# Feed-forward of an encoder on Trainium2: tokens on partitions, 256x1024 weight tiles, and Strassen's seven products in tiles 4 and 6 of each eight

## The chip, the cores and the metric

The kernel runs on one core of one Trainium2 chip. The metric is the device time of one execution in microseconds. An execution of the kernel before takes 2321.56 us (median of 3 runs, 2321.46 to 2324.35).

## What is computed

An encoder of two layers over x of 256 tokens x 2048, all in float32. Each layer is a norm, an attention (layer 0: neighbourhood attention with 16 heads; layer 1: dilated attention with 3 groups of 8 heads), a norm, and a feed-forward with squared ReLU; a last norm follows. The change is in the feed-forward, which is there twice:

```python
def rms_norm(x, g):
    y = xf * lax.rsqrt(jnp.mean(xf * xf, axis=-1, keepdims=True) + EPS)
    return (y * g.astype(jnp.float32)).astype(x.dtype)

def sq_relu_mlp(h, w1, w2):
    return jnp.square(jax.nn.relu(h @ w1)) @ w2        # w1: 2048 x 8192, w2: 8192 x 2048
...
        g, w1, w2 = ffns[i]
        x = x + sq_relu_mlp(rms_norm(x, g), w1, w2)
```

## The kernel before

All weights stream through the core once, in 400 blocks of 512 x 512 (1 MB each); 256 of them are the feed-forwards'. A block is one Step of a list, which is the program: `quarters` issues its matmuls in four parts, `tasks` are other matmuls put after a quarter (scores, transposes), `evac` reads finished sums, `post` follows. SyncE's queue loads a block into one of three buffers `w` (`load(i + 5)` after step i). `prep` cuts it in two halves of 128 x 1024: ScalarE rounds w into `wh` (line 104), VectorE subtracts to get the rest `wl` (line 105); there are four buffers of each, two steps' worth, and step i issues the cutting for step i + 2. Each engine takes its instructions in the order written here. Activations are cut into two parts in the same way, and a product is wh with both parts of the activation and wl with the first.

There are two forms of product. `gemm_cols` (lines 134 and 136) holds the weights still and gives out[columns, tokens]: 16 pairs of one matmul with 512 columns (both parts of the tokens) and one with 256. `gemm_rows` with `products` (lines 155 to 157) holds the activations still and gives out[tokens, columns]: 24 matmuls of 512 columns. The feed-forward (`ffn`) goes through the 8192 hidden columns in four groups of 2048: 16 blocks of the first product by `gemm_cols`, whose result, after ReLU and square, is at once hT, the left side of the second product; then 16 blocks of the second by `gemm_rows`. Sums lie in three pairs of PSUM banks, and two single banks serve transposes and scores. A norm's transposes (line 194) turn x, four of 128 x 128 at a time. `rows_apart` and `finish` end the kernel: the first half of the tokens is finished while the second half is multiplied.

## Time and profile before

| | |
|---|---|
| median of the runs | 2321.56 us |
| profiled execution, first to last instruction (no other time of it is listed) | 2320.3 us |
| TensorE busy (matmul) | 2300.7 us, 99% |
| VectorE busy | 1406.0 us, 61% |
| ScalarE busy | 1092.6 us, 47% |
| GpSimd busy | 0.7 us |
| bytes moved by DMA | 430.36 MB, 185 GB/s |
| granted TensorE clock, mean | 0.999 |

The span is cut in stages: up to 407 us layer 0's attention, to 1120 us its feed-forward, to 1601 us layer 1's attention, then its feed-forward and the last norm. Matmuls are pipelined, so the time from the start of one to the start of the next tells what it costs in a stream, and its own duration tells how long its result takes.

### The profile page before, as it was taken

Reading aid. Unit: us, or ns where it says so; the run is one execution under the profiler, and the core shown is the slowest. Engines: PE = TensorE matmul, PEld = TensorE weight load, DVE = VectorE, ACT = ScalarE, POOL = GpSimd, SP = SyncE. Lnnn points to the kernel's source line nnn. Section 1 sums busy time; section 2 is a strip of 40 time slices with the busy share of each in tenths; the row PEclk is TensorE's granted clock in tenths of the full one; section 3 lists DMA queues with packets and bytes.
Section 4 is the critical chain, followed back from the end, with each engine's and each line's share of the span. In section 5 each row is a group of like instructions: output and inputs, shape, how many; then the busy total and the mean of one; then the engine's idle time right before and its main releaser. Section 6 shows DMA issues by size and latency. Waiting matters only on the chain.

```text
span 2320.3 us, 29178 instructions
## 1 busy us (share of the span) xinstructions
PE 2300.7 (99%) x11956; PEld 1963.1 (85%) x11956; DVE 1406.0 (61%) x1635; ACT 1092.6 (47%) x1390; POOL 0.7 (0%) x6
## 2 busy tenths in 40 slices
PE   8999999999999999999999999999999999999998
PEld 7888888888888888888888888888888888888886
DVE  6666765654555555566777667756654654555654
ACT  6444545543443453455444544445543543543443
POOL 0000000000000000000000000000000000000000
PEclk9999999999999999999999999999999999999999
DMA  7555655555555555555555545454555555555553
GB/s 248 169 175 176 191 182 170 182 197 200 182 187 194 185 196 189 193 181 188 189 179 184 177 164 181 164 181 169 191 192 193 182 200 187 189 187 200 200 192 135
DMA packets 73862, 430.36 MB, mean 185 GB/s; under 512 B 19776, under 2 KB 20352, under 8 KB 22528
## 3 DMA queue, kind: packets, MB, share of 16 engines
q1 hardware_dynamic: 73056, 426.80, 54.3%
q8 instruction: 93, 1.52, 0.3%
q10 hardware_dynamic: 672, 1.70, 0.2%
q14 instruction: 41, 0.34, 0.0%
HBM read 426.38 MB, written 2.10 MB: 185 GB/s over the span
## 4 chain that ended last, share of the span: by engine, by line
PE 98%; DMA 1%; DVE 1%; ACT 0%; issue 0%; SPq 0%; ACTq 0%; DVEq 0%
PE acc L134 33%; PE acc L136 17%; PE acc L156 15%; PE acc L155 15%; PE acc L157 15%; PE misc L194 1%; DMA bias<-in_rpb_dram 0%; PE misc L111 0%; PE misc L110 0%; PE misc L109 0%; DVE wl L105 0%; PE misc L593 0%; PE misc L553 0%; PE misc L380 0%; ACT wh L104 0%
## 5 line engine op out<-in xcount | busy, mean ns | idle before, releaser
L105 DVE TENSOR_TENSOR wl<-w,wh 128x1024 fp32r<-128x1024 f32 (+1 forms) x802 | 972.8, 1221 | 735.8 <-ACT wh L104 733.6
L104 ACT CAST wh<-w 128x1024 fp32r<-128x1024 f32 (+1 forms) x802 | 834.9, 1049 | 936.9 <-PE acc L157 460.2
L134 PE MATMUL acc<-xT,wh 128*128 128x512 f32 x3328 | 1178.5, 399 | 0.9 <-ACT wh L104 0.9
L136 PE MATMUL acc<-xT,wl 128*128 128x256 f32 x3328 | 935.0, 281 | 2.3 <-DVE wl L105 2.3
L134 PEld LDWEIGHTS acc<-xT,wh 128*128 128x128 f32 x3328 | 626.4, 188 | 150.4 <-ACT wh L104 1.9
L136 PEld LDWEIGHTS acc<-xT,wl 128*128 128x128 f32 x3328 | 629.8, 189 | 3.7 <-DVE wl L105 3.2
L155 PE MATMUL acc<-wh,hT 128*128 128x512 f32 x1024 | 399.5, 390 | 0.0
L156 PE MATMUL acc<-wl,hT 128*128 128x512 f32 x1024 | 399.0, 390 | 0.0
L157 PE MATMUL acc<-wh,hT 128*128 128x512 f32 x1024 | 398.9, 390 | 0.0
L157 PEld LDWEIGHTS acc<-wh,hT 128*128 128x128 f32 x1024 | 192.3, 188 | 39.9
L155 PEld LDWEIGHTS acc<-wh,hT 128*128 128x128 f32 x1024 | 192.3, 188 | 39.7
L156 PEld LDWEIGHTS acc<-wl,hT 128*128 128x128 f32 x1024 | 192.3, 188 | 39.4
L155 PE MATMUL acc<-wh,xT 128*128 128x512 f32 x320 | 126.7, 396 | 0.0
L156 PE MATMUL acc<-wl,xT 128*128 128x512 f32 x320 | 125.2, 391 | 1.1 <-DVE wl L105 1.1
L157 PE MATMUL acc<-wh,xT 128*128 128x512 f32 x320 | 124.9, 390 | 0.0
L144 ACT COPY b<-acc 128x512 f32<-128x512 f32 x104 | 60.7, 586 | 64.8 <-PE acc L136 59.1
L146 DVE TENSOR_TENSOR z<-acc,b 128x512 f32<-128x512 f32 x104 | 71.5, 691 | 25.8 <-ACT b L144 25.2
L155 PE MATMUL acc<-wh,oT 128*128 128x512 f32 x192 | 76.6, 399 | 0.0
L157 PE MATMUL acc<-wh,oT 128*128 128x512 f32 x192 | 75.0, 391 | 0.0
L156 PE MATMUL acc<-wl,oT 128*128 128x512 f32 x192 | 74.9, 390 | 0.0
L156 PEld LDWEIGHTS acc<-wl,xT 128*128 128x128 f32 x320 | 60.2, 188 | 13.1 <-DVE wl L105 1.8
L157 PEld LDWEIGHTS acc<-wh,xT 128*128 128x128 f32 x320 | 60.1, 188 | 12.5
(123 smaller groups left out, 1044.9 us busy)
## 6 DMA issues: line engine op xcount, KB each, us to landing
w<-in_ffn_w_dram SPq DMA_DIRECT2D x256, 1024.0 KB, 4.8
w<-in_dil_wqkv_dram SPq DMA_DIRECT2D x72, 1024.0 KB, 4.8
w<-in_na_wqkv_dram SPq DMA_DIRECT2D x47, 1024.0 KB, 4.9
w<-in_na_wo_dram SPq DMA_DIRECT2D x16, 1024.0 KB, 4.9
w<-in_dil_wo_dram SPq DMA_DIRECT2D x8, 1024.0 KB, 4.8
bias<-in_rpb_dram SPq DMA_DIRECT2D x32, 96.0 KB, 8.7
out_dram<-x SPq DMA_DIRECT2D x8, 256.0 KB, 2.5
x<-in_x_dram SPq DMA_DIRECT2D x3, 512.0 KB, 7.8
```

Of the source, the lines that this page charges most:

```text
L104: nc.scalar.copy(dst_hi, src)
L105: nc.vector.tensor_tensor(out=dst_lo, in0=src, in1=dst_hi.bitcast(F32), op=ALU.subtract)
L134: nc.tensor.matmul(o, s.hi[a // 2][:, a % 2, cs], xt.rearrange("p h t -> p (h t)"), start=first, stop=False)
L136: nc.tensor.matmul(o[:, :T], s.lo[a // 2][:, a % 2, cs], xt[:, 0, :], start=False, stop=last)
L144: nc.scalar.copy(b, acc[j][:, :, T:])
L146: nc.vector.tensor_tensor(out=z, in0=acc[j][:, :, :T], in1=b, op=ALU.add)
L155: nc.tensor.matmul(o, xh, wh, start=start, stop=False)
L156: nc.tensor.matmul(o, xh, wl, start=False, stop=False)
L157: nc.tensor.matmul(o, xl, wh, start=False, stop=stop)
L194: nc.tensor.transpose(self.tp[:, a, tb * P:(tb + 1) * P], x[:, tb, kt * P:(kt + 1) * P], ident)
```

## The change

Both products of the feed-forward now hold the activations still (tokens on partitions). A Step is a tile of 256 x 1024 weights, four blocks of 128 x 512 in `w`, loaded by two DMAs of 512 KB. Each group of 2048 hidden columns is four runs of eight such tiles: two runs for the first product, two for the second; a run (`gemm_pair`) sums 2048 x 1024 weights into up to eight PSUM banks. Its tiles are of kind "s" (24 matmuls, as `gemm_rows`) or, for tiles 4 and 6 of the eight (`FF_PAIRS`, counted from 0: 3 and 5), "x": Strassen's seven products (Winograd's form), 21 matmuls. For an x tile the activations have three sums more (`sums_and_parts`), the weights four: VectorE adds `sums`, ScalarE rounds them into `hs`, VectorE subtracts to get `ls` (`prep_x`). The products with sums go to four banks "1", "6", "7", "5", which `begin` puts together in C after the last x tile; `end` adds the four banks of the plain sums ("2", "4", "S", "3") in the last tile. After a run of the first product C holds the hidden values with tokens on partitions: ScalarE applies 1/rms with ReLU and the square during tile 0 of the next run (`squared_relu`), four groups of four transposes follow in its tiles 1 and 2 (into the spare banks), and hT is cut from them (`post`). In the first norm of a feed-forward 1/rms is no longer spread over columns. Sums, subtractions and C are VectorE's alone.

The rest of the diff gives the buffers other pools: eight banks as one PSUM tile, of which the attention uses six in pairs and two singly as before, and SBUF pools that are begun for the attention or the feed-forward. The core of it:

```diff
+    def prep(i, n):
         if i >= len(steps):
             return
         s = steps[i]
-        hi = hlpool.tile([P, 2, 512], F32R, name="wh", tag="wh")
-        lo = hlpool.tile([P, 2, 512], F32R, name="wl", tag="wl")
-        part = s.w[:, 2 * u:2 * u + 2, :]
-        if i:
-            split(hi, lo, part)
+        if s.kind == "x":
+            prep_x(s, n)
...
+    def prep_x(s, n):
+        w = s.w
+        if n == 0:
+            t = s.sums = part.pool.tile([P, 4, 512], F32, name="sums", tag="sums", bufs=1)
+            add(nc.vector, t[:, 0:2, :], w[:, 1:3, :], w[:, 0, :].unsqueeze(1).to_broadcast([P, 2, 512]))
+            add(nc.vector, t[:, 2, :], t[:, 1, :], w[:, 1, :])
+            add(nc.vector, t[:, 3, :], t[:, 2, :], w[:, 3, :])
+        elif n == 1:
+            hi, lo = two_parts(s, 1)
+            split(hi, lo, w[:, 2:4, :])
+            s.hs = part.pool.tile([P, 4, 512], F32R, name="hs", tag="hs", bufs=2)
+            nc.scalar.copy(s.hs, s.sums)
+        elif n == 2:
+            ls = part.pool.tile([P, 4, 512], F32R, name="ls", tag="ls", bufs=2)
+            subtract(nc.vector, ls, s.sums, s.hs.bitcast(F32))
+            for a in range(4):
+                s.hi[4 + a], s.lo[4 + a] = s.hs[:, a, :], ls[:, a, :]
         else:
-            for a in range(2):
-                split(hi[:, a], lo[:, a], part[:, a])
-        s.hi[u], s.lo[u] = hi, lo
+            hi, lo = two_parts(s, 0)
+            split(hi[:, 1, :], lo[:, 1, :], w[:, 1, :])
     def block(w, k, c):
...
+        order, ps.order = ps.order, ps.order[4:] + ps.order[:4]
+        ps.spare = order[4:]
+        return {q: order[n] for n, q in enumerate(("2", "4", "S", "3", "1", "6", "7", "5"))}
...
+    STD = {(0, 0): "2", (0, 1): "3", (1, 0): "4", (1, 1): "S"}
...
+        def product(bank, a, b, last):
+            if not q:
+                q.update({k: banks[:, n, :] for k, n in sum_banks().items()})
+            three(q[bank], a, b, bank not in touched, last)
+            touched.add(bank)
+        X = (("1", "A11", 2), ("2", "A12", 3), ("6", "S2", 6), ("7", "S3", 4), ("5", "S1", 5), ("4", "A22", 7),
+             ("3", "S4", 1))
...
+            loads = [(w[k, 2 * cp + c].rearrange("p (a n) -> p a n", n=512)[:, 2 * u:2 * u + 2, :],
+                      2 - 2 * c, 4 - 2 * c) for c in (1, 0)]
+            if kind == "x":
+                def quarter(s, m, pair=pair, n=n):
+                    for bank, a, b in X[2 * m:2 * m + 2]:
+                        product(bank, left(pair, a), (s.hi[b], s.lo[b]), n == first_x[-1] and bank in "1567")
+            else:
+                def quarter(s, m, pair=pair, n=n):
+                    tb, c = ((0, 0), (1, 0), (1, 1), (0, 1))[m]
+                    for kk in range(2):
+                        b = 2 * (1 - c) + kk
+                        a = (("A11", "A12"), ("A21", "A22"))[tb][kk]
+                        product(STD[tb, c], left(pair, a), (s.hi[b], s.lo[b]), n == len(order) - 1 and kk == 1)
+            s = Step(kind, loads, quarter)
...
+        def begin(m):
+            if m == 0:
+                C = q["C"] = part.pool.tile([P, 4, 512], F32, name="C", tag="C")
+                nc.scalar.copy(C[:, 0, :], q["1"])
+                q["U"] = scratch([P, 512], "U")
+                subtract(nc.vector, q["U"], q["6"], C[:, 0, :])
+            elif m == 1:
+                subtract(nc.vector, q["C"][:, 2, :], q["U"], q["7"])
+            elif m == 2:
+                add(nc.vector, q["C"][:, 1, :], q["U"], q["5"])
+            else:
+                add(nc.vector, q["C"][:, 3, :], q["C"][:, 2, :], q["5"])
+        def end(m):
+            C = q["C"]
+            if m == 0:
+                add(nc.vector, C[:, 0, :], C[:, 0, :], q["2"])
+            elif m == 1:
+                subtract(nc.vector, C[:, 2, :], q["4"], C[:, 2, :])
+            elif m == 2:
+                add(nc.vector, C[:, 3, :], C[:, 3, :], q["S"])
+            else:
+                add(nc.vector, C[:, 1, :], C[:, 1, :], q["3"])
+        s = made[first_x[-1] + 1]
+        for m in range(4):
+            s.after[m].append(lambda m=m: begin(m))
+            if not split_end:
+                made[-1].after[m].append(lambda m=m: end(m))
+        finish(made, q)
...
+    def sums_and_parts(raw, t, half, sums):
+        c = scratch([P, 3, P], "c")
+        a11, a21, a12, a22 = raw[:, 0, :P], raw[:, 0, P:], raw[:, 1, :P], raw[:, 1, P:]
+        subtract(nc.vector, c[:, 0, :], a11, a21)
+        subtract(nc.vector, a21, a21, a22)
+        subtract(nc.vector, c[:, 1, :], a11, a21)
+        subtract(nc.vector, c[:, 2, :], a12, c[:, 1, :])
+        hi, lo = (t[:, 2 * half:2 * half + 2, h, :] for h in range(2))
+        nc.scalar.copy(hi, raw)
+        nc.scalar.copy(sums[:, 0], c)
+        subtract(nc.vector, lo, raw, hi.bitcast(F32))
+        subtract(nc.vector, sums[:, 1], c, sums[:, 0].bitcast(F32))
...
+    FF_PAIRS = (3, 5)
+    FF_ORDER = [("x" if k in FF_PAIRS else "s", k) for k in range(8)]
+    FF_LAST = [FF_ORDER[k] for k in (0, 1, 3, 2, 5, 4, 6, 7)]
...
-                def done(zs, c=c, hT=hT):
-                    t = hT[c] = big.tile([P, 4, 2, T], F32R, name="hT", tag="big")
-                    for z in zs:
-                        nc.vector.scalar_tensor_tensor(
-                            out=z, in0=z, scalar=0.0, in1=norm.bc.unsqueeze(1).to_broadcast([P, 2, T]),
-                            op0=ALU.max, op1=ALU.mult)
-                        nc.scalar.activation(z, z, AF.Square)
-                    for j, z in enumerate(zs):
-                        split(t[:, 2 * j:2 * j + 2, 0, :], t[:, 2 * j:2 * j + 2, 1, :], z)
-                gemm_cols(w1, (4 * g + c) * 512, norm.xT, 4, done)
+            hT, sums = [None] * 4, {}
+            def hidden(made, q, cp, hT=hT, sums=sums):
...
+                def squared_relu(tb, n):
+                    c = q["C"][:, 2 * tb + n, :]
+                    nc.scalar.activation(c, c, AF.Relu, scale=norm.r[:, tb:tb + 1])
+                    nc.scalar.activation(c, c, AF.Square)
+                for m, (tb, n) in enumerate(((0, 0), (1, 0), (1, 1), (0, 1))):
+                    at_after(i, m, lambda tb=tb, n=n: squared_relu(tb, n))
+                for r in range(4):
+                    held = {}
+                    def pe(r=r, held=held):
+                        held["t"] = t = ps.misc()
+                        for a in range(2):
+                            f = 2 * r + a
+                            for tb in range(2):
+                                nc.tensor.transpose(t[:, a, tb * P:(tb + 1) * P],
+                                                    q["C"][:, 2 * tb + f // 4, f % 4 * P:(f % 4 + 1) * P], ident)
+                    def post(r=r, held=held):
+                        c, half, pair = 2 * cp + r // 2, r % 2, 4 * cp + r
+                        if half == 0:
+                            hT[c] = opool.tile([P, 4, 2, T], F32R, name="hT", tag="o")
+                        if pair in FF_PAIRS:
+                            raw = scratch([P, 2, T], "h")
+                            nc.scalar.copy(raw, held["t"])
+                            sums[pair] = part.pool.tile([P, 2, 3, P], F32R, name="hs", tag="hsum", bufs=len(FF_PAIRS))
+                            sums_and_parts(raw, hT[c], half, sums[pair])
+                        else:
+                            to = hT[c][:, 2 * half:2 * half + 2]
+                            split(to[:, :, 0, :], to[:, :, 1, :], held["t"])
+                    at(i + 1 + r // 2, pe, post, quarter=r % 2 * 2)
...
+                gemm_pair(w1, 2 * g + cp, norm.xT, norm.sums, FF_ORDER, lambda made, q, cp=cp: hidden(made, q, cp))
...
-            out_rows(w2g, hT, 4, next_norm if last else None, next_done if last else None)
...
+                def rows(tb):
+                    to = x[:, tb, cp * 1024:(cp + 1) * 1024]
+                    add(nc.vector, to, to, both(q, tb))
+                made[-1].evac.append(lambda: rows(1))
+                made[-1].evac.append(lambda: rows(0))
...
+            if i == 0 and n in (1, 2):
+                prep(1, 2 * n - 1)
+            elif i in (1, 2):
+                if n == 2:
+                    prep(i + 2, 1)
+            elif i and n < 3:
+                prep(i + 2, n)
...
-        prep(i + 2, 1)
+            prep(2, 1)
+        prep(i + 2, 3)
```

How this moves instructions, at three places. **VectorE, at the start of the second product of a group.** Before (hT is the last cut of the hidden values, line 105 `split`, line 271 the addition to x):

```order
L471 SCALAR_TENSOR_TENSOR z<-z,rbc 128x512 x2
L105 TENSOR_TENSOR hT<-z,hT 128x2x256 x2
L105 TENSOR_TENSOR wl<-w,wh 128x1024 x7
L271 TENSOR_TENSOR x<-x,acc 128x512 x2
L105 TENSOR_TENSOR wl<-w,wh 128x1024 x8
```

Now, in tiles 1 and 2 of the second product's first run, from `ls` of tile 3 on (line 133 subtracts, line 191 is `split`; c and h are the sums of the activations and their raw values, hs and hT here their two parts):

```order
L133 TENSOR_TENSOR ls<-sums,hs 128x2048
L133 TENSOR_TENSOR c<-h 128x128
L133 TENSOR_TENSOR h<-h 128x128
L133 TENSOR_TENSOR c<-h 128x128
L133 TENSOR_TENSOR c<-h,c 128x128
L133 TENSOR_TENSOR hT<-h,hT 128x2x256
L133 TENSOR_TENSOR hs<-c,hs 128x384
L191 TENSOR_TENSOR wl<-w,wh 128x512
L191 TENSOR_TENSOR hT<-banks,hT 128x2x256
L191 TENSOR_TENSOR wl<-w,wh 128x1024
L191 TENSOR_TENSOR hT<-banks,hT 128x2x256
L191 TENSOR_TENSOR wl<-w,wh 128x1024
```

Where VectorE had a cut of weights alone there now stands a 2048-column subtraction and six instructions on the activations, and the cut of the last transposes (the second hT out of banks) is behind all of them.

**ScalarE, at the same change from the first product to the second.** Before (line 474 is the square, 104 the casts):

```order
L474 ACTIVATE z<-z 128x512 x2
L104 CAST hT<-z 128x2x256 x2
L104 CAST wh<-w 128x1024 x39
```

Now, in tile 0 of the next run and the start of tile 1 (lines 681 and 682 are ReLU and square, 190 the casts, 176 the cast of the weight sums):

```order
L681 ACTIVATE C<-C,rstd 128x512
L682 ACTIVATE C<-C 128x512
L681 ACTIVATE C<-C,rstd 128x512
L682 ACTIVATE C<-C 128x512
L190 CAST wh<-w 128x1024
L681 ACTIVATE C<-C,rstd 128x512
L682 ACTIVATE C<-C 128x512
L681 ACTIVATE C<-C,rstd 128x512
L682 ACTIVATE C<-C 128x512
L190 CAST wh<-w 128x1024
L190 CAST hT<-banks 128x2x256
L190 CAST wh<-w 128x1024
```

The two casts of tile 2 stand behind four and behind eight passes over C.

**TensorE, in tile 3 of the second product's first run**, the first x tile, with the engines that each matmul waits for (lines 195 to 197 are `three`). Before, a block of the second product waits only for its weights:

```order
L155 MATMUL acc<-wh,hT 128x512 [waits Activation_49]
L156 MATMUL acc<-wl,hT 128x512 [waits DVE_49]
L157 MATMUL acc<-wh,hT 128x512
L155 MATMUL acc<-wh,hT 128x512
L156 MATMUL acc<-wl,hT 128x512
```

Now, from the third of the seven products on (banks "6", "7", "5", and the first of "4"):

```order
L195 MATMUL banks<-hs 128x512 [waits Activation_49]
L196 MATMUL banks<-ls,hs 128x512 [waits DVE_49]
L197 MATMUL banks<-hs 128x512
L195 MATMUL banks<-hs 128x512 [waits DVE_49]
L196 MATMUL banks<-ls,hs 128x512
L197 MATMUL banks<-hs 128x512
L195 MATMUL banks<-hs,hT 128x512 [waits DVE_49]
L196 MATMUL banks<-ls,hT 128x512
L197 MATMUL banks<-hs,hT 128x512
L195 MATMUL banks<-hs,hT 128x512
```

Product "6" waits for `hs` and `ls`; "7" and "5" each wait once more for VectorE, which frees their banks when it has cut the third and the fourth group of transposes.

## Rows read from the trace of the kernel before

**Rows 1.** The page's head: busy time by engine, granted clock by slice

```profile
span 2320.3 us, 29178 instructions
PE 2300.7 (99%) x11956; PEld 1963.1 (85%) x11956; DVE 1406.0 (61%) x1635; ACT 1092.6 (47%) x1390; POOL 0.7 (0%) x6
...
PEclk9999999999999999999999999999999999999999
```

**Rows 2.** Waits, whole span: who waited for whom, us in total, times, longest

```profile
ACT wh L104 <- PE acc L157: 460.2, 292, 2.2
ACT wh L104 <- PE acc L134: 452.4, 269, 3.5
...
PE acc L136 <- DVE wl L105: 2.3, 3, 0.8
PE acc L156 <- DVE wl L105: 1.1, 2, 0.6
```

**Rows 3.** Windows of the two feed-forward stages: busy time by engine, clock, DMA

```profile
407.00:1119.57 712.57, 712.57 (x3622) 605.45 (x3620) 406.27 (x421) 332.03 (x386) 0.00 (x0) 1.00 0.56 189
...
1601.35:2320.00 718.65, 709.96 (x3597) 602.94 (x3595) 403.05 (x417) 328.68 (x381) 0.00 (x0) 1.00 0.54 187
```

**Rows 4.** Timeline of TensorE at the edges of products: start us, us, what

```profile
584.27 0.39 PE L134 MATMUL acc<-xT,wh 128*128 128x512 f32 x1
...
674.71 0.40 PE L155 MATMUL acc<-wh,hT 128*128 128x512 f32 x1
...
761.78 0.39 PE L134 MATMUL acc<-xT,wh 128*128 128x512 f32 x1
...
1601.35 0.39 PE L134 MATMUL acc<-xT,wh 128*128 128x512 f32 x1
...
1691.56 0.39 PE L155 MATMUL acc<-wh,hT 128*128 128x512 f32 x1
```

**Rows 5.** Timeline of TensorE around four transposes (line 194)

```profile
376.12 0.60 PE L194 MATMUL misc<-ident,x 128*128 128x128 f32 x4
376.47 0.48 PE L155 MATMUL acc<-wh,oT 128*128 128x512 f32 x1
376.79 0.39 PE L156 MATMUL acc<-wl,oT 128*128 128x512 f32 x1
```

**Rows 6.** Groups by line and shape: count, busy us, mean ns, idle before

```profile
L105 DVE TENSOR_TENSOR wl<-w,wh 128x1024 fp32r<-128x1024 f32 x798 | 970.2, 1223 | 735.8 <-ACT wh L104 733.6
L104 ACT CAST wh<-w 128x1024 fp32r<-128x1024 f32 x798 | 832.6, 1051 | 936.9 <-PE acc L157 460.2 <-PE acc L134 452.4 <-issue 9.2
...
L105 DVE TENSOR_TENSOR hT<-z,hT 128x512 fp32r<-128x512 f32 x64 | 41.4, 689 | 38.7 <-ACT hT L104 38.7
...
L474 ACT ACTIVATE z<-z 128x512 f32<-128x512 f32 x64 | 39.5, 633 | 60.6 <-DVE z L471 60.6
...
L104 ACT CAST hT<-z 128x512 fp32r<-128x512 f32 x64 | 36.0, 610 | 0.0
...
L194 PE MATMUL misc<-ident,x 128*128 128x128 f32 x128 | 20.3, 283 | 5.9 <-DMA x<-in_x_dram 5.9
...
L105 DVE TENSOR_TENSOR oT<-misc,oT 128x256 fp32r<-128x256 f32 x16 | 6.7, 418 | 0.0
...
L690 ACT ACTIVATE x<-x,fr 128x512 f32<-128x512 f32 x4 | 2.7, 716 | 1.4 <-DVE fr L680 1.4
...
L260 DVE TENSOR_TENSOR ru<-ru,ms 128x2 f32<-128x2 f32 x4 | 0.7, 162 | 0.1
```

**Rows 7.** Timelines of VectorE and ScalarE: instructions that follow one another

```profile
436.04 1.29 DVE L105 TENSOR_TENSOR hT<-z,hT 128x512 fp32r<-128x512 f32 x2 [1.21 <-ACT hT L104]
437.52 2.36 DVE L105 TENSOR_TENSOR wl<-w,wh 128x1024 fp32r<-128x1024 f32 x2 [0.18 <-ACT wh L104]
...
436.44 2.00 ACT L104 CAST wh<-w 128x1024 fp32r<-128x1024 f32 x2
```

**Rows 8.** Timeline of the end: VectorE in `finish`

```profile
2305.91 0.69 DVE L669 TENSOR_TENSOR x<-x,acc 128x512 f32<-128x512 f32 x1 [3.13 <-PE acc L157]
...
2308.92 0.74 DVE L687 SCALAR_TENSOR_TENSOR x<-x,fr,gf 128x512 f32<-128x512 f32 x1
```

**Rows 9.** DMA issues: size, median us to landing

```profile
w<-in_ffn_w_dram SPq DMA_DIRECT2D x256, 1024.0 KB, 4.8
```

More of the change, by code (lines that the diff above doesn't have):

```diff
@@ L341, in qk @@
         def qk(self, which):
-            t = [mid.tile([P, 4, T], F32R, name="qk", tag="mid") for _ in range(2)]
+            t = [part.pool.tile([P, 4, T], F32R, name="qk", tag="mid", bufs=9) for _ in range(2)]
             setattr(self, which, t)
@@ L382, in s2_post @@
         def s2_post(self, h):
-            t = [tmp.tile([P, 2, T], F32R, name="pT", tag="p", bufs=5) for _ in range(2)]
+            t = [part.pool.tile([P, 2, T], F32R, name="pT", tag="p", bufs=5) for _ in range(2)]
             split(t[0], t[1], self.pt)
@@ L482, in tile_encoder, with both @@
+            def both(q, tb):
+                return q["C"][:, 2 * tb:2 * tb + 2, :].rearrange("p a n -> p (a n)")
+            for cp in range(2):
+                end = last and next_norm() in fin and cp == 1
+                gemm_pair(w2g, cp, hT, sums, FF_LAST if end else FF_ORDER,
+                          lambda made, q, cp=cp: residual(made, q, cp), split_end=end)
     ffn(norms[1], ins["ffn0_w1"], ins["ffn0_w2"], lambda: norms[2], begin_norm(2, True))
+    parts[len(steps)] = "attention"
@@ L736, in tile_encoder @@
     for i, s in enumerate(steps):
+        now["i"] = i
+        if i in parts:
+            part.begin(parts[i])
         if i == 1:
@@ L764, in tile_encoder @@
         if i < len(steps) - 2:
-            s.w = s.hi = s.lo = None
+            s.w = s.hi = s.lo = s.hs = s.sums = s.pair = None
+    part.end()
 _WEIGHTS = ["na_wqkv", "na_wo", "ffn0_w1", "ffn0_w2", "dil_wqkv", "dil_wo", "ffn1_w1", "ffn1_w2"]
```

307 lines of the change are left out of this document (204 added, 103 removed).

## The prediction

> **What bounds the kernel now.** I read the page's head first: TensorE is busy for 2300.7 of 2320.3 us at full granted clock, VectorE for 1406.0, ScalarE for 1092.6 [rows 1]. Busy alone would not prove the bound, so the waits came next: the two longest waits of TensorE on a cut weight are 2.3 and 1.1 us over the whole span, while ScalarE waits 460.2 and 452.4 us for TensorE to give weight buffers back [rows 2]. So the cutting of weights follows TensorE, and the time is the number of matmuls times their spacing. The stretches by stage say how much of it the change can touch: the two feed-forwards last 712.57 and some 710 us (the fourth stretch of 718.65 less the tail), without a gap on TensorE, with VectorE busy 406.27 of 712.57 [rows 3].
>
> **TensorE, term by term.** The edges of one group (g = 1, first feed-forward) are 584.27, 674.71 and 761.78 [rows 4]. The first product takes 90.44 us for 16 blocks, the second 87.06 for 16, which is 87.06 / 384 = 0.2267 us per 512-column matmul. A block with tokens on partitions is 24 such matmuls, 5.441 us; the first product's form (16 pairs of 512 and 256 columns) takes 90.44 / 16 = 5.653.
>
> First, the first product changes form: 16 x (5.653 - 5.441) = 3.4 us less per group. Second, 8 of the group's 32 tiles are of kind "x" with 7 products instead of 8, 21 matmuls: 8 x 3 x 0.2267 = 5.4 us less. Third, hidden values now come out with tokens on partitions and must be turned: 64 new groups of four transposes, 8 per group of 32 tiles. In the stream of matmuls four transposes stand between 376.12 and 376.79 with one 512-column matmul of 0.227 behind them, so four cost 0.67 - 0.22 = 0.45 us [rows 5]; 8 x 0.45 = 3.6 us more. Together 177.50 becomes 24 x 5.441 + 8 x 4.761 + 3.6 = 172.27, 5.23 less, times 8 groups 41.8.
>
> Corrections: the first group of each feed-forward runs its first product in 90.2 us with three groups of four norm matmuls inside (its edges, 1601.35 and 1691.56 [rows 4]), so 88.85 without them and 1.6 less to win, twice: -3.2. The row of 1/rms is no longer spread for norms 1 and 3 (one group of four each): 0.9 won. Net 39.5 us.
>
> The four transposes are the one term for which the case has a contrary rule. The row gives 283 ns for one alone but 0.45 us for four in the stream, at full clock [rows 5, 6]. The Trainium skill (TensorE: Matmul & The Clock Gate, Part 4: PE-mode transpose) says that a transpose takes about 275 ns in a kernel and does not count as activity for the clock; by it the 256 would cost 70 us in place of 28.8. The trace agrees with it for one alone, not for their spacing. I take the spacing.
>
> **What VectorE and ScalarE must do instead.** Durations [rows 6]: VectorE takes 689 ns for 512 columns and 1223 for 1024; ScalarE 610 and 1051 for casts, 633 for a square, 716 for a scaled 512-column pass. Not shown are 2048 columns (by the slope, an estimate of 2.30 us on VectorE and 1.93 on ScalarE), 384 and 128 columns (0.55 and 0.29, between the 418 of 256 columns and the 162 of two). Two instructions in a row without a wait between them take less than their sum: 2.36 for two of 1223, 1.29 for two of 689, 2.00 for two casts of 1051 [rows 7], so each that follows without a wait costs 0.09 to 0.10 less.
>
> An "s" tile needs two 1024-column subtractions, as before. An "x" tile needs on VectorE sums (1.14 + 0.69 + 0.69), wl (1.14), ls (2.30), half a wl (0.60), and some 0.7 of waiting for ScalarE's copy hs: about 7.3 us against 4.76 of TensorE. The two x tiles of an eight are spread by an s tile, so the account must be kept by tile. Over a group VectorE has 24 x 2.36 + 8 x 7.3 + C (32 instructions of 0.65) + hidden (6 x 0.65 + 2 x 2.4) + rows (4 x 1.15) = 149 of 172 us: it fits on average, 86%.
>
> Where it piles up is the eight behind one of the first product, whose tiles 0 to 2 carry the squared ReLU, the transposes and their cuts. The walk of the second product's first eight (time 0 is the start of its tile 0; tiles 1, 2, 3 start at 5.44, 11.78, 18.12): ScalarE has wh 1.05 and four pairs of scaled ReLU and square at 1.3 with the two casts for tile 2 among them, and ends the second cast at 8.35, 2.7 later than its buffer came free (5.44 + 0.2). VectorE cuts that at 9.6, then the sums to 12.1, hT of the first transposes and wl to 13.9, ls (behind ScalarE's hs, 12.1 to 14.05) to 16.4, the chain of sums of the activations with its two cuts to 18.9, half a wl 19.5, then hT of the third transposes at 20.1, wl 21.4, hT of the fourth at 22.0. Tile 3 is an x tile and writes into the banks that held these transposes: product "7" at 18.12 + 3 x 0.68 = 20.16, in time; product "5" at 20.84, and its bank comes free at 22.0: **TensorE waits 1.2 us**. The order shows a wait of its own on VectorE at both. Without the overlap of following instructions the same walk gives 21.2 and 23.3, 2.5 us of waiting. In the first product's second eight the special pair is the fourth, whose bank is free after a mere copy; there the walk ends with ls of tile 5 at 30.0 for a matmul at 29.9: 0.1, or 1.6 without overlap. The other two eights carry no transposes, and VectorE is over a microsecond ahead. So waiting costs 1.25 x 8 = 10 us by the overlapped rows, 4.0 x 8 = 32 by the rows added up, and nothing if the chain before it is 1.2 us shorter than I add it up. I take 10, since following instructions overlap in every pair shown. Behind TensorE's wait stand only its own later matmuls; ScalarE and VectorE then wait for its buffers as before.
>
> Edges: at the end finish for the first half of the tokens takes VectorE from 2305.91 to 2309.66 [rows 8], and the second now follows 2.72 us (half a tile) behind in place of 5.4, so it starts 1.0 late: +1.0. At the change to layer 1 the first transposes wait for two 1024-column additions to x: +0.4. Weight loads are as large as before, as two of 512 KB; 1024 KB lands in 4.8 us [rows 9], and from the release of a buffer to the first use of its next tile the walk leaves at least 7 us: nothing. The attention parts keep their matmuls and their order: nothing.
>
> Sum: 2320.3 - 39.5 + 10 + 1.4 = 2292.2 for the profiled execution; the median of the runs is 1.3 above the span shown, so **2293.5**.
>
> **Rivals.** (a) No waiting at all: 2283.5. For it: ScalarE's casts of the tile after may slip earlier than I put them, and 1.2 us is little. (b) VectorE's instructions cost their full rows at each hand-over, since most have a wait of their own: 32 us, 2315.5. (c) Slower: VectorE becomes the bound in every eight. If no part of an x tile's preparation overlaps (sums 2.60, wh 1.05, wl 1.22, hs 1.93, ls 2.30, half a wh 0.62, half a wl 0.69), it takes 10.4 us; two x and two s tiles then take 2 x (10.4 + 2.45) = 25.7 against 20.4 of TensorE, 5.3 late less some 2 of slack, 3.3 x 32 eights = 106 us: 2389. It decides from about 8.7 us per x tile, where 32 x 2 x 0.7 us or so are lost on top of 2293.5. Against it: ScalarE's casts depend on nothing of VectorE's but hs, and the 2.36 of two. (d) Slower too: transposes that do not follow one another at 0.11 us but at their 283 ns add 256 x 0.17 = 43.6: 2337; the stretch at 376 speaks against it. That mechanism is the rule of the Trainium skill named above (TensorE: Matmul & The Clock Gate, Part 4); with its 275 ns the sum would be 2335. That the change leaves the matmuls as they are is excluded: the order has 7488 matmuls of 512 columns with tokens on partitions, 64 x 3 fewer than 64 + 256 blocks of 24 would have.
>
> **How the numbers follow.** A measurement of this kernel tells about 0.2% (4.6 us) from no change: below 2316.9 is faster, above 2326.2 slower. Chances: the forecast (waits of about 10, 2287 to 2303) 0.48; (a) 0.20; (b), 2303 to 2317, 0.17; between (b) and (c), within the bound, 0.05; (c) 0.08; (d) 0.02. Faster 0.85, same 0.05, slower 0.10. The range for 8 in 10 reaches from (a) less 4.5 for the terms read to 0.1 us per group, 2279, to (b), 2316.
>
> **What would show it.** The first product's 16 tiles at 5.44 us each and x tiles at 4.76; four transposes in 0.45; a wait of TensorE of 1 to 1.5 us, 8 times, for VectorE's cut hT in the first x tile of the second product's first eight; VectorE busy about 80% in the feed-forward; ls at 2.3 us. Wrong would be: waits at every x tile on ls or sums (rival c), weights that land late, or a granted clock below full.

## The result and the profile after

The changed kernel takes 2309.88 us (median of 4 runs, 2308.40 to 2311.07) against 2322.22 us of the kernel before (median of 4, 2321.46 to 2324.35): a ratio of 0.9944, 95% interval 0.993 to 0.9959. It is faster by 12.3 us, where 28 were forecast; the profiled execution has a span of 2306.6 us where the sum gave 2292.2.

The page's head answers to [rows 1]; engines with busy time, share and instructions:

```profile
span 2306.6 us, 28352 instructions
PE 2273.0 (99%) x10988; PEld 1898.0 (82%) x10988; DVE 1758.8 (76%) x2082; ACT 1217.7 (53%) x1526; POOL 0.7 (0%) x6
```

VectorE has 353 us more to do and ScalarE 125; TensorE stays at 99%. So the missing gain must lie in TensorE's own chain, and the waits come next, as in [rows 2] (who waited for whom, us in total, times, longest). In the changed kernel lines 195 to 197 are the three matmuls of a product, 191 a cut (wl, hT), 133 and 136 VectorE's subtractions and additions, 384 a norm's transposes, 427 its row of 1/rms, 410 the scaled copy gx of norm 2:

```profile
PE banks L195 <- DVE hT L191: 6.9, 8, 0.9
PE banks L196 <- DVE ls L133: 3.3, 3, 1.4
PE banks L384 <- DVE gx L410: 2.0, 2, 1.9
PE banks L427 <- DVE gx L410: 1.1, 1, 1.1
PE banks L384 <- DVE x L136: 0.8, 2, 0.4
```

The first row is the wait that was forecast. Of the others, 7.2 us, the forecast had only 0.4, for the additions to x (the last row). The windows of the stages, as in [rows 3] (length, then busy time of each engine), first that of the second attention before the change, then the three stages after it:

```profile
1119.57:1601.35 481.78, 481.78 (x2633) 416.15 (x2632) 330.54 (x432) 224.91 (x294) 0.00 (x0) 1.00 0.51 176
```

```profile
404.93:1109.35 704.42, 698.40 (x3129) 572.57 (x3128) 574.68 (x627) 389.12 (x442) 0.00 (x0) 1.00 0.60 192
1109.35:1595.57 486.22, 482.78 (x2641) 416.43 (x2640) 338.70 (x451) 230.32 (x306) 0.00 (x0) 1.00 0.51 174
1595.57:2306.00 710.43, 696.11 (x3113) 571.09 (x3111) 576.43 (x633) 389.22 (x445) 0.00 (x0) 1.00 0.60 190
```

Stage by stage, before to after: up to the first feed-forward 407.00 to 404.93; first feed-forward 712.57 to 704.42 (8.15 less); second attention 481.78 to 486.22 (4.44 **more**, in a stage that the change hardly touches, though two groups of norm 2's transposes, eight matmuls or 0.9 us, now stand behind its edge and no longer ahead of it: x2641 for x2633); second feed-forward with the end 718.95 to 711.03 (7.92 less). A full group went from 177.50 to 174.54 us, where the sum had 172.27 + 1.25. VectorE is busy 574.68 of 704.42 us in a feed-forward, 82%.

Now the places, on TensorE's timeline (start, us, what; in brackets what it waited for), with VectorE's cut beside the first:

```profile
513.39 0.40 PE L197 MATMUL banks<-hs 128*128 128x512 f32 x1
514.66 0.50 PE L195 MATMUL banks<-hs,hT 128*128 128x512 f32 x1 [0.86 <-DVE hT L191]
```

```profile
513.92 0.68 DVE L191 TENSOR_TENSOR hT<-banks,hT 128x512 fp32r<-128x512 f32 x1
```

That is product "5" of the first x tile in the second product's first eight: 1.27 from start to start in place of 0.23, released by the cut of the fourth transposes, which ends at 514.60. Eight times; the tile lasts 5.98 where the other x tiles last 4.86, so 1.12 lost each. The next three rows are the first matmul of an x tile without any wait, of the s tile behind it and of the tile after that:

```profile
607.09 0.39 PE L195 MATMUL banks<-wh,xT 128*128 128x512 f32 x1
611.94 0.39 PE L195 MATMUL banks<-wh,xT 128*128 128x512 f32 x1
617.39 0.39 PE L195 MATMUL banks<-wh,xT 128*128 128x512 f32 x1
```

The s tile has its 5.44 to 5.45; the x tile takes 4.85 to 4.86 for 21 matmuls, 0.2312 each and not the 0.2267 of [rows 4]. And at the entry of the second attention a group of norm 2's transposes, and then two windows (0.57 and 1.00 are the granted clock):

```profile
1125.29 0.65 PE L384 MATMUL banks<-ident,x 128*128 128x128 f32 x4 [1.86 <-DVE gx L410]
```

```profile
1126.00:1130.00 4.00, 4.00 (x15) 3.41 (x14) 2.76 (x6) 1.86 (x3) 0.00 (x0) 0.57 0.26 109
1130.00:1595.57 465.57, 465.57 (x2550) 402.20 (x2549) 321.46 (x418) 219.46 (x284) 0.00 (x0) 1.00 0.52 176
```

The same matmul (line 136 before, 222 after) stands 13.48 us behind the edge of the stage in the kernel before and 20.25 behind it now:

```profile
1133.05 0.28 PE L136 MATMUL acc<-xT,wl 128*128 128x256 f32 x1
```

```profile
1129.60 0.35 PE L222 MATMUL banks<-xT,wl 128*128 128x256 f32 x1
```

Of these 6.8 us, 0.9 are the two groups that have moved. The other 5.9 are lost: waits for VectorE's work on norm 2, then nearly 4 us at 0.57 of the clock, that is mostly at its lower level of 1.2 GHz, right behind the longest of them.

### The profile page after: what moved, and what is told of

Read it like the earlier page. It is cut to its first block, busy times and chain, and to the rows that moved or that the text cites. A ratio compares the mean times of both kernels' runs of the same rounds, so it can differ in the third digit from the quotient of the medians.

```text
span 2306.6 us, 28352 instructions
## 1 busy us (share of the span) xinstructions
PE 2273.0 (99%) x10988; PEld 1898.0 (82%) x10988; DVE 1758.8 (76%) x2082; ACT 1217.7 (53%) x1526; POOL 0.7 (0%) x6
## 4 chain that ended last, share of the span: by engine, by line
PE 87%; DVE 5%; ACT 5%; issue 2%; DMA 1%; SPq 0%; ACTq 0%; DVEq 0%
PE banks L195 22%; PE banks L196 22%; PE banks L197 22%; PE banks L220 13%; PE banks L222 6%; ACT wh L190 2%; DVE wl L191 1%; DVE sums L136 1%; DVE ls L133 1%; ACT C L681 1%; ACT hs L176 1%; PE banks L694 1%; PE banks L384 1%; ACT C L682 0%; DMA bias<-in_rpb_dram 0%
## 5 line engine op out<-in xcount | busy, mean ns | idle before, releaser
L220 PE MATMUL banks<-xT,wh 128*128 128x512 f32 x1280 | 455.6, 399 | 0.5 <-ACT wh L190 0.4
L195 PE MATMUL banks<-wh,xT 128*128 128x512 f32 x1152 | 453.7, 394 | 0.0
L197 PE MATMUL banks<-wh,xT 128*128 128x512 f32 x1152 | 449.3, 390 | 0.0
L196 PE MATMUL banks<-wl,xT 128*128 128x512 f32 x1152 | 448.6, 389 | 0.6 <-DVE wl L191 0.6
L222 PE MATMUL banks<-xT,wl 128*128 128x256 f32 x1280 | 358.5, 280 | 2.3 <-DVE wl L191 2.3
L195 PE MATMUL banks<-wh,hT 128*128 128x512 f32 x832 | 327.2, 393 | 0.0
L197 PE MATMUL banks<-wh,hT 128*128 128x512 f32 x832 | 324.4, 390 | 0.0
L196 PE MATMUL banks<-wl,hT 128*128 128x512 f32 x832 | 323.8, 389 | 0.0
L220 PEld LDWEIGHTS banks<-xT,wh 128*128 128x128 f32 x1280 | 241.6, 189 | 55.6 <-ACT wh L190 1.5
L197 PEld LDWEIGHTS banks<-wh,xT 128*128 128x128 f32 x1152 | 216.2, 188 | 45.8
L195 PEld LDWEIGHTS banks<-wh,xT 128*128 128x128 f32 x1152 | 216.5, 188 | 42.7
L222 PEld LDWEIGHTS banks<-xT,wl 128*128 128x128 f32 x1280 | 242.4, 189 | 3.7 <-DVE wl L191 3.4
L176 ACT CAST hs<-sums 128x2048 fp32r<-128x2048 f32 x64 | 122.5, 1914 | 156.5 <-DVE sums L136 156.5
L197 PEld LDWEIGHTS banks<-wh,hT 128*128 128x128 f32 x832 | 156.2, 188 | 33.0
L195 PEld LDWEIGHTS banks<-wh,hT 128*128 128x128 f32 x832 | 156.3, 188 | 31.3
L133 DVE TENSOR_TENSOR ls<-sums,hs 128x2048 fp32r<-128x2048 f32 x64 | 146.7, 2292 | 43.6 <-ACT hs L176 43.6
```

The costliest lines, as they stand in the source:

```text
L133: engine.tensor_tensor(out=out, in0=a, in1=b, op=ALU.subtract)
L176: nc.scalar.copy(s.hs, s.sums)
L195: nc.tensor.matmul(o, left[0], right[0], start=start, stop=False)
L196: nc.tensor.matmul(o, left[0], right[1], start=False, stop=False)
L197: nc.tensor.matmul(o, left[1], right[0], start=False, stop=stop)
L220: nc.tensor.matmul(o, s.hi[a][:, cs], xt.rearrange("p h t -> p (h t)"), start=first, stop=False)
```

## The experiments

Ratios are to the kernel before, with their interval; "less" and "more" are against the changed kernel's 2309.88 us unless said otherwise. In e1 and e5 only the times of tiles count.

**e3, one part alone: no seven-product tile.**

```diff
-    FF_PAIRS = (3, 5)
+    FF_PAIRS = ()
...
+            if not first_x:
...
+                nc.vector.tensor_copy(q["C"][:, (0, 2, 3, 1)[m], :], q[("2", "4", "S", "3")[m]])
```

> One part of the change alone: tokens on partitions in all tiles, transposed hidden values, 256x1024 weight tiles, but no seven-product tile (all 32 tiles of a group are s tiles, C is copied from the banks). By rows: a group is 32 x 5.44 + 8 x 0.465 = 177.8 us, so each feed-forward is 4 x 177.8 plus the norm matmuls = some 714 to 716, against 712.6 before and 704.4 with x tiles; no wait for hT. If the 3.4 us at x tiles of the first feed-forward's last eight come from x tiles' cuts, they are gone. The entry of the second attention (6.8 us lost in its first 21 us): if VectorE's additions to x and C make it late it stays, and the time is 2327 to 2332; if the x tiles' cuts make it late it is gone, and the time is 2320 to 2326.

Measured 2329.85 us, ratio 1.0032 (1.002 to 1.0044). The stages:

```profile
405.40:1120.10 714.70, 714.27 (x3226) 591.35 (x3225) 396.41 (x395) 335.60 (x378) 0.00 (x0) 1.00 0.61 189
1120.10:1604.80 484.70, 481.24 (x2641) 415.10 (x2640) 335.93 (x443) 228.33 (x302) 0.00 (x0) 1.00 0.50 175
```

So the rest of the change costs 7.5 us by itself, and the seven products win 20.0 us, 0.31 per x tile, where 64 x 3 x 0.2267 = 43.5 less 10 of waits was the sum. The entry of the second attention is slow here too (gx, 2.1 and 1.1 us, in its waits): the x tiles don't cause that. VectorE's passes over C and its 1024-column additions to x, which both kernels have, are left, and e4 tests them. The granted clock did not fall in this run, nor in e2, behind the same waits.

**e2, the wait for hT: products "7" and "5" last.**

```diff
-        X = (("1", "A11", 2), ("2", "A12", 3), ("6", "S2", 6), ("7", "S3", 4), ("5", "S1", 5), ("4", "A22", 7),
-             ("3", "S4", 1))
+        X = (("1", "A11", 2), ("2", "A12", 3), ("6", "S2", 6), ("4", "A22", 7), ("3", "S4", 1), ("7", "S3", 4),
+             ("5", "S1", 5))
```

> Only the order of the products within an x tile changes: 1, 2, 6, 4, 3, 7, 5 in place of 1, 2, 6, 7, 5, 4, 3. My theory: TensorE waits 8 x 1.04 us in the second product's first eight since product '5' wants its bank before VectorE has cut the fourth transposes; product '5' is now two products (1.36 us) later, so the wait goes and nothing takes its place: 8.3 us less, 2301.6 us, 0.9964 of the changed kernel's time and 0.991 of the kernel before. Rival: VectorE is late as a whole there and the wait turns up at the next cut (ls of that tile, or wl of the tiles behind): 2308 to 2311.

Measured 2299.73 us, ratio 0.9901 (0.9888 to 0.9915): 10.2 us less. No wait for hT is left. At the place shown above (VectorE's last cut of hT, then product "5"):

```profile
515.34 0.68 DVE L191 TENSOR_TENSOR hT<-banks,hT 128x512 fp32r<-128x512 f32 x1
```

```profile
516.45 0.39 PE L195 MATMUL banks<-hs,hT 128*128 128x512 f32 x1
```

The cut ends 0.43 us before the product starts, and all eight tiles fall from about 5.98 to 4.86: 9.0 of the 10.2 us. 1.5 us more came from the second attention, 484.70 after 486.22 us, where the clock stayed full. The rival, a VectorE that is late as a whole, is out.

**e4, the hand-over to norm 2.**

```diff
-                    nc.vector.tensor_scalar(out=gx.rearrange("p (r s j) -> p r s j", s=4, r=4), in0=src,
-                                            scalar1=g, scalar2=None, op0=ALU.mult)
+                    nc.scalar.activation(gx.rearrange("p (r s j) -> p r s j", s=4, r=4), src, AF.Copy, scale=g)
...
+                if last and cp == 1:
+                    def chunk(n):
+                        for tb in range(2):
+                            cs = slice((2 + n) * 512, (3 + n) * 512)
+                            add(nc.vector, x[:, tb, cs], x[:, tb, cs], q["C"][:, 2 * tb + n, :])
+                    made[-1].after[1].append(lambda: chunk(0))
+                    made[-1].evac.append(lambda: chunk(1))
```

> Only the hand-over from the first feed-forward to the second attention changes: the scaled and reordered copy of norm 2's transposes is made by ScalarE in place of VectorE (32 instructions of 0.48 us), and the additions to x of the last columns go by 512 columns, the first half of them two quarters of a tile earlier. My theory: VectorE's backlog there costs 3.4 us in the first feed-forward's last eight and 6.8 us at the entry of the second attention (waits for gx, then 3.7 us at a granted clock of 0.57 behind the longest of them); with it lightened 6 to 9 us are won, 2301 to 2304. Rival: the casts of ScalarE become late in its place (it has its own 2.1 us of casts per step there): 2308 to 2312.

Measured 2301.89 us, ratio 0.9912 (0.9897 to 0.9927): 8.0 us less. First feed-forward and second attention:

```profile
405.64:1107.72 702.08, 698.16 (x3129) 572.70 (x3128) 571.39 (x620) 391.89 (x450) 0.00 (x0) 1.00 0.60 192
1107.72:1588.60 480.88, 480.55 (x2641) 415.25 (x2640) 334.87 (x444) 233.12 (x314) 0.00 (x0) 1.00 0.51 176
```

5.3 us come from the entry, 2.3 from the feed-forward's last eight (its x tiles 5.14 and 4.96, after 6.59 and 5.88); one wait of 0.3 us, now for ScalarE, is left at the entry. VectorE's backlog was the cause at both places. The edit makes two moves at once, and no run parts them; of the 5.3 us some 1.5 are the clock, which stays full here.

**e1 and e5, why an x tile takes 4.86 us.** Other operands, group by group, with the same matmuls and banks. The core of the edits, the first of e1, the second of e5:

```diff
+        if "w" in form:
+            X = tuple((b, a, {6: 2, 4: 3, 5: 2, 7: 3}.get(i, i)) for b, a, i in X)
+        if "t" in form:
+            X = tuple((b, {"S2": "A11", "S3": "A12", "S4": "A21"}.get(a, a), i) for b, a, i in X)
...
+                       {"A11": "S2", "A12": "S3", "S1": "S4", "A22": "S2"}.get(a, a) if "xs" in form else plain_t.get(a, a),
...
+                       {2: 6, 3: 7, 1: 5}.get(i, i) if "hs" in form else plain_w.get(i, i)) for b, a, i in X)
```

> This kernel changes operands, so its output is not the reference's: in the first feed-forward the seven products of an x tile take, in the second group, wh and wl in place of hs and ls as moving operand; in the third, slices of xT and hT in place of the sums of activations as stationary operand; in the fourth, both. In the second feed-forward the first group puts the products '1' and '2' last, and in the second group the s tiles (but the last of an eight) go round their four banks three matmuls at a time. Question: why an x tile takes 4.86 us for 21 matmuls and not 21 x 0.2267 = 4.76. Theory A, the moving operand hs/ls: x tiles of 4.76 in the second and fourth groups, 4.86 in the third. Theory B, the stationary operand xs: 4.76 or near in the third and fourth, 4.86 in the second. Theory C, the banks taken three matmuls at a time: 4.86 in all four, and the s tiles of the second feed-forward's second group rise from 5.44 towards 5.57 (24 x 0.232). If it is none of these, all x tiles stay at 4.86 and those s tiles at 5.44. Waits on cuts are counted apart.

Measured (first matmul of a tile to the first of the next, tiles without waits): 4.85 to 4.86 with wh in place of hs, 4.85 to 4.86 with xT in place of xs, **4.76 with both**. With the s tiles' banks taken three matmuls at a time an s tile stays at 5.44, so the banks are not it; the order "1" and "2" last leaves x tiles at 4.86 (and brings waits of up to 4 us, since "5" is wanted earlier still). Theories A and B each fall as put: either special operand alone does all of it. The x tile of the fourth group, its first matmul and the first behind it:

```profile
946.89 0.39 PE L195 MATMUL banks<-wh,xT 128*128 128x512 f32 x1
951.65 0.39 PE L195 MATMUL banks<-wh,xT 128*128 128x512 f32 x1
```

> Again a kernel with other operands, so its output is not the reference's. x tiles keep their 21 matmuls and seven banks. First feed-forward (an unused tile of 1 KB lies ahead of sums, hs and ls): first group as it was; second group only product '5' (three matmuls) keeps its own moving operand hs/ls, all else takes wh/wl and xT or hT; third group only product '6' keeps its sum of activations as stationary operand; fourth group nothing keeps either. Second feed-forward (the unused tile is 3.06 KB): first group as it was; second group all seven products take hs/ls as moving operand; third group all take sums of activations as stationary operand; fourth group all take both. In the runs so far either special operand alone gave 4.86 and none gave 4.76. Theory A, the place of the operand in the memory: each special matmul costs 0.005 to 0.006 more whatever stands beside it, so 'only 5' and 'only 6' give 4.77 to 4.79, and the second feed-forward's last three groups 4.87 or more. Theory B, the change from one pair of operand tiles to another: one special product costs a few matmuls behind it as well, 4.80 to 4.83, and tiles that read all from hs/ls or all from sums of activations fall to 4.76 to 4.80. Theory C, the address within the memory by some alignment: the unused tile changes 4.86 in one or both first groups.

Measured: only "5" special 4.79, only "6" special 4.78 to 4.79, neither 4.76; all from hs with xT 4.90, all from sums of activations with wh 4.90, **all from both 4.77 to 4.80**. The unused tiles of 1 KB and 3.06 KB leave the x tiles of the first groups at 4.86 and 4.84. In these two pairs an x tile starts and ends, all hs with xT first, then all hs with xs:

```profile
1785.19 0.40 PE L195 MATMUL banks<-hs,xT 128*128 128x512 f32 x1
1790.09 0.40 PE L195 MATMUL banks<-wh,xT 128*128 128x512 f32 x1
...
2136.53 0.39 PE L195 MATMUL banks<-hs,xs 128*128 128x512 f32 x1
2141.32 0.39 PE L195 MATMUL banks<-wh,xT 128*128 128x512 f32 x1
```

Neither theory holds as put: A missed the last, B the two of 4.90. What is slow is a matmul whose two operands are of different kinds, 0.233 us in a stretch of such matmuls; two ordinary ones or two special ones take 0.227 in a stretch of their own. Three mixed matmuls cost 0.02 to 0.03, more than their own 3 x 0.006, so some neighbours pay too. That is why the six matmuls of products "6" and "7" take 1.39 us in the changed kernel, 0.232 each, though both of their operands are special (the first of the six, and the first behind them):

```profile
608.46 0.39 PE L195 MATMUL banks<-hs,xs 128*128 128x512 f32 x1
609.85 0.39 PE L195 MATMUL banks<-hs,xT 128*128 128x512 f32 x1
```

The kinds differ in where the tiles lie, which e8 tests.

**e6, both edits together** (those of e2 and e4).

> The two edits that won time put together: product '5' and '7' last, and ScalarE's copy with the earlier additions at norm 2. If they act at different places they add: 2309.9 - 10.2 - 8.0 = 2291.7, 0.987 of the kernel before. They share one place, the first feed-forward's last eight (x tiles 6.60 and 5.88 in the changed kernel, 7.41 and 5.08 with the first edit, 5.14 and 4.96 with the second), so up to 2 us may be missing: 2291 to 2294.

Measured 2293.45 us, ratio 0.9873 (0.986 to 0.9887): 16.4 us less, so of 18.2 all but 1.8 add. This is now the forecast's 2293.5, by chance: its sum had 10 us for the wait that is gone here and nothing for the spacing that is still there.

**e8 and e10, the same kernel with tiles at other places in the memory.** e8 in all stages, e10 in the feed-forwards alone. The edit of e10, beside those of e6:

```diff
             part.begin(parts[i])
+            if parts[i][0] == "f":
+                pad = part.pool.tile([P, 8], F32, name="pad", tag="pad")
+                nc.gpsimd.memset(pad[:, 0:1], 0.0)
```

> The kernel with both edits, and nothing changed but where tiles lie in the memory: in the kernels so far wh, wl, xT and hT start at 32 bytes past a multiple of 64 in each partition (160 past one of 512), while hs, ls, the sums of activations, C, ident and x start at a multiple of 64. An unused tile of 288 bytes (32 in the second feed-forward) ahead of the tiles of each stage, and the one-element tile ahead of x, put all of them at 32 past a multiple of 64. The runs before showed 0.2267 us per matmul where both operands are of one kind, (wh, xT) or (hs, sums of activations), and 0.232 where they are mixed. Theory A, the offset: x tiles fall from 4.86 to 4.76 and four transposes from 0.465 to some 0.45, 64 x 0.1 + 64 x 0.015 = 7 us, so 2286.4; if the offset counts by 512 and not by 64, in the first feed-forward alone, 2290. Theory B, the distance or region of the memory (the special tiles lie above 160000 bytes, the others below 157000): nothing changes, 2293.

Measured 2292.57 us, ratio 0.9868 (0.9851 to 0.9884), no gain over e6 that can be told, where theory A had 2286.4. The x tiles without waits did fall to 4.76, in both feed-forwards, so with 32 bytes as with 288. Each feed-forward won 1.8 to 1.9 us; the eights with transposes gave part of the 0.1 per x tile back, since an x tile that is sooner waits longer for ls (4.82 to 5.07, where e6 has 4.84 to 5.04). The other half of theory A missed: with C and ident at one offset too, an s tile with two groups of transposes did not fall from its 6.37 but rose to 6.41. Here are the first matmul of such a tile and the first behind it (line 197 is line 195 of the other kernels), and the second attention:

```profile
635.05 0.39 PE L197 MATMUL banks<-wh,xT 128*128 128x512 f32 x1
641.45 0.39 PE L197 MATMUL banks<-wh,xT 128*128 128x512 f32 x1
```

```profile
1102.73:1586.09 483.36, 483.03 (x2641) 416.65 (x2640) 334.69 (x444) 233.02 (x314) 0.00 (x0) 1.00 0.51 175
```

The second attention grew from 480.90 to 483.36 us, and the first ended 1.6 us later, which is within what it varies between kernels (below).

> The kernel with both edits (2293.45 us) and an unused tile of 32 bytes ahead of the feed-forwards' own tiles only. In the run that moved tiles in all stages each feed-forward lost 1.9 us or so (x tiles 4.86 to 4.76, given back in part in the eights with transposes), but the first attention grew by 1.6 us and the second by 2.5, where x, ident and the attention's own tiles were moved too. If those moves cost the attention its time, it is back here: 2293.45 - 3.8 = 2289.6. If the attention is slower whatever is moved in it (an effect of what runs ahead of it), 2292 to 2294.

Measured 2289.11 us, ratio 0.9854 (0.9839 to 0.9868): 4.3 us less than e6, 3.9 of them in the feed-forwards. An x tile from its first matmul to the first of the s tile, and the three stages:

```profile
597.53 0.39 PE L195 MATMUL banks<-wh,xT 128*128 128x512 f32 x1
602.29 0.39 PE L195 MATMUL banks<-wh,xT 128*128 128x512 f32 x1
```

```profile
406.79:1102.09 695.30, 694.81 (x3129) 572.83 (x3128) 570.51 (x620) 391.54 (x450) 0.00 (x0) 1.00 0.62 194
1102.09:1582.99 480.90, 480.56 (x2641) 415.26 (x2640) 334.85 (x444) 233.18 (x314) 0.10 (x1) 1.00 0.52 176
1582.99:2287.00 704.01, 692.88 (x3113) 571.22 (x3111) 575.88 (x633) 389.02 (x445) 0.00 (x0) 1.00 0.60 191
```

The second attention is back at 480.90. So theory A holds for the matmuls of the feed-forward's x tiles: there the offset of the two operands within 64 bytes counts, since 32 bytes do all of it and e5's multiples of 64 next to nothing. In the attention, other tiles or x and ident at the new offset cost 2.5 us. The traces tell where: the projections' matmuls, 768 pairs of 512 and 256 columns by `gemm_cols`, take 268.1 us in e8 and in the kernel before, and 265.8 in e2, e3, e4, e6, e7, e10 and e11 alike (added up from one start to the next). Their own operands, wh, wl and xT, did not move in e8, so their offset against each other is not all that counts; and in the first attention, where nothing differs between these kernels, such pairs take 181.8 to 183.3. Which of the moved tiles does it, and why, was not tried.

**e11, the last eight as sssxxsss.**

```diff
-    FF_LAST = [FF_ORDER[k] for k in (0, 1, 3, 2, 5, 4, 6, 7)]
+    FF_LAST = [FF_ORDER[k] for k in (0, 1, 2, 3, 5, 4, 6, 7)]
```

> The same, and in the last eight of the second feed-forward the x tiles at places 3 and 4 in place of 2 and 4 (sssxxsss for ssxsxsss). There TensorE waited 1.3 us for ls of the x tile at place 2, whose cuts fall into tile 0, beside 3.6 us of additions. One tile later they fall behind these: 1.3 us less than the run before it. Rival: two x tiles in a row make ls of the second late by as much (the third of three in a row came 2.3 us late in the first eights of the run with a third x tile, the second of three mostly in time): no change.

Measured 2288.69 us, ratio 0.9852 (0.9836 to 0.9869): 0.4 less than e10, not to be told from nothing. The first x tile is in time, the second now waits 0.75 us for ls, where in e10 the first waited 1.10: the rival, mostly.

**e7 and e9, a third x tile in the first product.** Both have the edits of e2 and e4; e9 also moves the additions for sums to GpSimd.

```diff
+    FF_FIRST = [("x" if k in (3, 4, 5) else "s", k) for k in range(8)]
...
-                gemm_pair(w1, 2 * g + cp, norm.xT, norm.sums, FF_ORDER, lambda made, q, cp=cp: hidden(made, q, cp))
+                gemm_pair(w1, 2 * g + cp, norm.xT, norm.sums, FF_FIRST, lambda made, q, cp=cp: hidden(made, q, cp))
...
-            add(nc.vector, t[:, 2, :], t[:, 1, :], w[:, 1, :])
+            add(nc.gpsimd, t[:, 2, :], t[:, 1, :], w[:, 1, :])
...
```

> The kernel with both edits, and in the first product of each group a third x tile (pairs 3, 4 and 5, so three x tiles in a row). 16 more x tiles at 5.44 - 4.86 = 0.58 us are worth 9.3 us if VectorE keeps up: 2282.4. It tests the rival in which VectorE is the bound: an x tile adds 4.9 us of cutting to 2.4, and three in a row ask 22 us of VectorE in the three tiles ahead of them, which last 15.7 to 17.6; the lead of about 7 us covers that where no transposes stand (first eight), and not in the second eight, whose tiles 1 and 2 also carry 5 us of hidden values. I expect waits for ls of 2 to 4 us in each of the 8 second eights, 16 to 32 us in all, so 2298 to 2314, slower than with two x tiles.

Measured 2342.45 us, ratio 1.0086 (1.0072 to 1.0099), 49.0 us slower than e6 and 28 beyond the expected range. Its waits:

```profile
PE banks L196 <- DVE ls L133: 26.2, 18, 1.6
PE banks L196 <- DVE wl L191: 16.6, 26, 1.4
```

The three x tiles of a second eight take 5.28, 6.04 and 8.31 us in place of 4.86, and even in a first eight, where I had expected time enough, the third takes 7.2 to 7.5. VectorE becomes the bound when three x tiles follow one another, although over the first feed-forward it is busy only 602.33 of 721.68 us, 83%.

> The kernel with a third x tile in the first product (2342.45 us), with the three additions that make sums on GpSimd in place of VectorE: 2.6 us less of VectorE per x tile, 7.3 to 4.7. Theory: the 49 us by which the third x tile made it slower than the kernel with two (2293.45), in place of 9.3 faster, are VectorE's; with 4.7 us per x tile against 4.86 of TensorE the waits go and the time is 2284 to 2290. Rival: GpSimd's additions take so long, or VectorE's slow so much beside them, that the waits stay or grow: 2330 or more. No trace here shows an addition on GpSimd.

Measured 2440.67 us, ratio 1.0508 (1.0492 to 1.0524): the rival. GpSimd's groups:

```profile
L136 POOL TENSOR_TENSOR sums<-sums,w 128x512 f32<-128x512 f32 x160 | 281.7, 1761 | 12.5
L136 POOL TENSOR_TENSOR sums<-w 128x1024 f32<-128x1024 f32 x80 | 212.4, 2654 | 1902.1 <-DMA w<-in_ffn_w_dram 674.9 <-DVE ru L471 508.7 <-DVE wl L191 500.3
```

2654 + 2 x 1761 ns = 6.2 us per x tile, more than the 4.86 of TensorE, where VectorE takes 1218 + 2 x 692 ns = 2.6. VectorE's own cuts of 1024 columns took 1395 ns on average beside it, after 1222. The Trainium skill (SBUF — State Buffer, Who interferes with whom) says that a VectorE instruction with two inputs in SBUF contends with a GpSimd instruction that reads SBUF; the slower cuts agree with it, and no run here tells that from another cause. Not all of the 147 us over e6 are the two engines' own: beside the waits for them the granted clock fell to its lower level in 21 places, 99 us in all (mean 0.977, where e6 has 0.998). By an estimate from these 99 us at half the speed, up to 50 are the clock's.

## Why the prediction came out as it did

**Right.** The first product's s tiles take 5.44 us; ls 2292 ns and hs 1914 ns (2.30 and 1.93 by the slope); VectorE is busy 82%; weights never come late. Above all the walk of VectorE found the wait, its place, its count and nearly its size: product "5" of the first x tile of the second product's first eight, eight times, 1.12 us for 1.25. e2 shows the mechanism by taking it away. Rival (d), transposes at 283 ns each, is out at 0.465 us for four (6.37 - 5.44 = 0.93 for two groups, at full clock). Rival (c), VectorE the bound, did not hold with two x tiles, and e7 shows how near it is.

**Wrong.** The sum was 14.4 us too low (2306.6 for 2292.2), and two of its steps failed.

The first is "7 products ... 8 x 3 x 0.2267": I priced an x tile's 21 matmuls at the spacing of matmuls with other operands. They came at 0.2312, 4.855 for 4.761: 64 x 0.094 = 6.0 us, and the s tile behind each takes 5.452 for 5.440, 0.8 more. e1, e5, e8 and e10 show that it goes with where the two operands lie and not with banks or order. Nothing in the trace of before showed hs or the sums of activations, so this price had to be an unknown with two bounds; I gave it one value.

The second is "Edges ... The attention parts keep their matmuls and their order: nothing", and with it "The other two eights carry no transposes". I had walked VectorE's work in two of a group's four eights, and not in the one eight and the entry where norm 2 has its transposes and puts its own work on VectorE, on top of C and of additions that had become twice as long. The first feed-forward's last eight lost 3.4 us (tiles of 7.03, 6.59 and 5.88 for 6.37, 4.86 and 4.86); the entry of the second attention 5.9 where I had 0.4, of which some 1.5 are the clock (486.22 against 484.70 us in e2 and e3, where the waits are the same and the clock stays full). e4 takes back 8.0 of it.

Smaller terms: four transposes 0.465 for 0.45 (64 x 0.015 = 1.0); ls of the second x tile in the first product's second eight, which the walk had 0.1 late and for which I charged nothing, 5.04 for 4.86 (8 x 0.18 = 1.4); the last eight of all, where the x tile at place 2 takes 6.28 for 4.86 as it waits for ls (1.4), and 0.3 at the end; the forecast wait 1.0 too dear. Against these the second attention's other matmuls came 2.3 us sooner in all, which is the 268.1 and 265.8 us of its projections (e10), and the first attention ended 2.1 us earlier; that end lies between 404.9 and 407.3 in kernels of this study that run it alike, so it is no part of the change. 6.0 + 0.8 + 3.4 + 5.5 + 1.0 + 1.4 + 1.7 - 1.0 - 2.3 - 2.1 = 14.4.

One reading of the prediction was wrong without consequence: the 2.3 and 1.1 us of [rows 2], which it calls the two longest waits, are totals of three and of two waits, the longest of them 0.8.

Rival (b), 2315.5, lies nearer to the time than the forecast, but not for its reason: the waits for hT were 9 us and not 32. The missing gain went to a spacing taken from other operands and to a stage edge that was not walked; with these and the counted wait undone (e10) the same change gives 33.8 us, 2289.11 against 2322.95.

## What to carry to other kernels

Busy shares hide where a helping engine piles up: 82% over a feed-forward hid a wait in every group and a broken stage edge, and three heavy tiles in a row broke it at 83%. So walk the helping engine tile by tile through every kind of stretch, the first and the last of a stage above all, where the next stage's work begins. When several results go to banks that others still hold, order the products so that those banks come last: here this was worth 9 us and cost nothing. A spacing read from the trace holds for the operands that it was read with; for new tiles keep a bound on either side.

## What was not expected of the hardware

In the feed-forward's tiles a matmul of 512 columns takes 0.227 us when both operands' tiles begin at the same offset within 64 bytes, and 0.233 when they do not; 32 bytes of padding moved the x tiles without waits from 4.86 to 4.76 us. In the attention the same kind of move cost 2.5 us, nearly all of it in matmuls whose own operands had not moved, and it did not help transposes, so no rule follows yet. The granted clock fell to 0.57 for 4 us behind a wait of 1.86 us that had two others of 0.2 and 1.1 us close before it, in the profiled run of the changed kernel; it fell there in e5 too, and not behind the same waits in e1, e2 and e3. GpSimd took 2.2 to 2.5 times as long as VectorE for the same additions (2654 for 1218 ns, 1761 for 692).
